# 96 gathered tokens instead of 80, a dense part 160 tokens wide, and another dealing out of the gather steps

## The chip, the cores and the metric

The kernel runs on one core of one Trainium2 chip. The time is that of one execution in device microseconds; lower is better. TensorE (PE) multiplies, VectorE (DVE) and ScalarE (ACT) do element work, GpSimd (POOL) issues the gathers, and the sequencer SP issues most of the plain loads. All transfers run on the core's 16 DMA engines.

## The reference, cut to what matters

The program is a small trunk of two layers on 256 tokens with 1024 features: a mixer, attention to a memory, and an expert part (`peer_ffn`), then a last norm. All is f32. The change concerns the expert part, in both layers alike. Each token has 8 heads, and each head picks 16 out of 16,384 experts, so 128 experts a token:

```python
eid = ...                                   # (tokens, 128) experts chosen
g = softmax(top) ...                        # (tokens, 128) their weights
act = gelu(einsum('td,ted->te', xb, u[eid]))
out = einsum('te,ted->td', g * act, v[eid])
```

`u` and `v` are tables of 16,384 rows of 1024 f32 per layer, 64 MiB each.

## The kernel before

**Two ways for the tokens.** The first `NG` = 80 tokens are *gathered*: for each, the 128 chosen rows of `u` and of `v` are fetched. The other `TD` = 176 tokens are *dense*: every expert is computed for them, and the weights of those that a token did not choose are zero. `GROUPS = ((0, 64), (64, 16))` divides the gathered tokens: 64 tokens whose 128 experts lie in 2 slots of 64 partitions, and 16 tokens with 8 slots of 16 partitions. One gather step takes one expert for each of 128 (token, slot) places, so a group of n tokens needs n steps with `u` and n with `v`; 80 + 80 = 160 steps a layer.

**The dense part** goes over the experts in 64 pairs of 128. For a `u` pair (`u_range`, matmuls at line 827) 1 MB of `peer_u` is loaded into a buffer `raw`, and 16 matmuls of 128 x 128 weights against the 176 dense tokens (`xd`) give the scores; ACT makes the gelu of them (line 833), for the first 20 pairs into `af`, for the others into `act`. The generator yields after each half pair. For a `v` pair (`v_pair`, matmuls at line 1134) 1 MB of `peer_v` is loaded, DVE multiplies the activations with the weights `gr` into `wt` (line 1130, three buffers), and 16 matmuls add to four banks `O`, which stay open through the whole stage. In the profile each f32 matmul is two instructions, 32 to a pair. `load` takes five `raw` buffers in turn; SP issues the loads.

**The gather steps** are the generator `gathered` (variable `bg`): each step issues an indirect load of 128 rows of 4 KB on POOL (`rows`, line 790; eight row buffers), and then one DVE instruction: with `u` rows a product with the token and its sum (line 797), with `v` rows a weighted add into `acc` (line 809, the first one line 807). The first 80 steps are those with `u`, the other 80 those with `v`. `turn[1]` counts the steps issued. At the end of a layer a matmul with `fold` adds the slots of `acc` up (line 1175).

**Order.** Within three stages DVE's order is the one written in the program, the rest is ordered by the compiler's planner. First, `choose` (top-k and the indices) is interleaved with `u` pairs: `interleave` calls one half pair for each 2.2 units of cost (`Q1`) that `choose` yields. What is left of the first 20 pairs runs with one gather step to each half pair (`steps`). Second, `spread` builds the dense weights from one-hot matmuls (line 1083), in groups of 16 dense tokens, 11 of them, and writes them to DRAM (`gd`); the next 20 `u` pairs run beside it, one half pair for each 1.7 units (`Q2`), and one gather step to two half pairs. Third, the v stage: 64 `v` pairs in the order of `order`, which are 6 of the first 20 (`NHEAD`, their weights already in `af`), then the others with the 14 remaining ones strewn in. Behind each `v` pair from 20 upwards one whole `u` pair follows, until the last 24 are used up. `gr` is read back from `gd` in pieces for 4 pairs (`weights_of`). After each `v` pair comes one gather step, after each fourth two: 80 in all. The steps that are then left run after the last pair, in `for _ in bg: pass`.

Of the kernel before, what the change touches and what calls it, by code (L numbers as in the profile page):

```python
# [28 lines left out]
NPAIR = 64  # L29
TG = 16  # L30
NFIRST = 20
NACT = 20

GROUPS = ((0, 64), (64, 16))
NG = sum(n for _, n in GROUPS)
TD = T - NG
NHEAD = 6
GQ = 4
Q1 = 2.2
Q2 = 1.7  # L40
# [28 lines left out]
def trunk(ctx: ExitStack, tc: tile.TileContext, a: dict, out: bass.AP, dbg=None):  # L69
# [37 lines left out]
    def bank():  # L107
        return ps.tile([P, 512], F32, name="b", tag="ps", bufs=2)
# [625 lines left out]
    def peer(l, sq, fill=None):  # L734
        with ExitStack() as es:
# [17 lines left out]
            gs_ = []  # L753
            for gn, (t0, n) in enumerate(GROUPS):
                xg = pp.tile([P, D], F32, name=f"xg{gn}", tag=f"ga{gn}")
# [15 lines left out]
            turn = [0, 0]  # L771


            def load(src):

                n = turn[0] % 5
                turn[0] += 1
                if n < 3:
                    raw = st.tile([P, 2048], F32, name="raw", tag="raw", bufs=3)
                else:  # L780
                    raw = cp.tile([P, 2048], F32, name="raw", tag=f"xT{n - 3}", bufs=1)
                nc.sync.dma_start(raw, src)
                return raw

            def rows(src, g, i):

                q = ("whi", "wlo")[turn[1] % 2]
                turn[1] += 1
                t = st.tile([P, D], F32, name="row", tag=q, bufs=4)
                nc.gpsimd.indirect_dma_start(t, None, src, bass.IndirectOffsetOnAxis(ap=g["gi"][:, i:i + 1], axis=0))  # L790
                return t

            def gathered():
                for g in gs_:
                    for i in range(g["n"]):
                        t = rows(u_rows, g, i)
                        nc.vector.tensor_tensor_reduce(t, t, g["xg"], 1.0, 0.0, OP.mult, OP.add, g["dots"][:, i:i + 1])  # L797
                        if i == g["n"] - 1:
                            nc.scalar.activation(g["dots"], g["dots"], AF.Gelu_apprx_tanh)
                            nc.vector.tensor_mul(g["gw"], g["gw"], g["dots"])  # L800
                        yield
                for gn, g in enumerate(gs_):
                    acc = g["acc"] = pp.tile([P, D], F32, name=f"acc{gn}", tag=f"ga{gn}")
                    for i in range(g["n"]):
                        t = rows(v_rows, g, i)
                        if i == 0:
                            nc.vector.tensor_scalar(acc, t, g["gw"][:, 0:1], None, op0=OP.mult)
                        else:
                            nc.vector.scalar_tensor_tensor(acc, t, g["gw"][:, i:i + 1], acc, op0=OP.mult, op1=OP.add)  # L809
                        yield  # L810
# [8 lines left out]
            def u_range(i, j):  # L819

                for i in range(i, j):
                    raw = load(a["peer_u"][l, i])
                    b = bank()
                    for c in range(2):
                        for k in range(KB):
                            o = c * 1024 + k * P
                            nc.tensor.matmul(b[:, c * TD:(c + 1) * TD], raw[:, o:o + P], xd[:, k], start=k == 0, stop=k == KB - 1)  # L827
                        if c == 1:
                            if i < NFIRST:
                                dst = af[:, 2 * i:2 * i + 2].rearrange("p c t -> p (c t)")  # L830
                            else:
                                dst = act[i] = pools["ex"].tile([P, 2 * TD], F32, name="act", bufs=NACT)
                            nc.scalar.activation(dst, b[:, :2 * TD], AF.Gelu_apprx_tanh)  # L833
                            done.append(dst)
                        yield
# [197 lines left out]
            us = u_range(0, NFIRST)  # L1033
            interleave(choose(), us, Q1)
            bg = gathered()

            def steps():
# [64 lines left out]
            us = u_range(NFIRST, NFIRST + NACT)  # L1102
# [10 lines left out]
            def weights_of(g):  # L1113
                if g < (NPAIR - NFIRST) // GQ:
                    gr[g] = vp.tile([P, TD // TG, GQ * 2 * TG], F32, name="gr", bufs=2)
                    nc.sync.dma_start(gr[g], gd[:, :, g * GQ * 2 * TG:(g + 1) * GQ * 2 * TG].rearrange("g p f -> p g f"))

            def v_pair(i, first, last):
                if i < NFIRST:
                    raw = load(a["peer_v"][l, i])  # L1120
                    wt = af[:, 2 * i:2 * i + 2]
                else:
                    g, j = divmod(i - NFIRST, GQ)
                    if j == 0:
                        weights_of(g + 1)
                    gv = gr[g][:, :, j * 2 * TG:(j + 1) * 2 * TG].rearrange("p g (c t) -> p c g t", c=2)
                    raw = load(a["peer_v"][l, i])
                    at = act.pop(i)
                    wt = vp.tile([P, 2, TD], F32, name="wt", bufs=3)
                    nc.vector.tensor_mul(wt.rearrange("p c (g t) -> p c g t", t=TG),  # L1130
                                         at.rearrange("p (c g t) -> p c g t", c=2, t=TG), gv)
                parts = [(c, j) for c in range(2) for j in range(KB)]
                for c, j in sorted(parts, key=lambda z: z[1]) if last else parts:
                    nc.tensor.matmul(O[j // 2][:, (j % 2) * TD:(j % 2 + 1) * TD], raw[:, c * 1024 + j * P:c * 1024 + (j + 1) * P],  # L1134
                                     wt[:, c], start=first and c == 0 and j % 2 == 0, stop=last and c == 1,
                                     skip_group_check=True)
                if last:
                    ready_sqrt(wt[:, 0, 0:1])


            order, late = list(range(NHEAD)), list(range(NHEAD, NFIRST))
            for i in range(NFIRST, NPAIR):
# [2 lines left out]
                    order.append(late.pop(0))  # L1145
            order += late
            us = u_range(NFIRST + NACT, NPAIR)
            with tc.manual_schedule(engines={nc.vector.engine}):
                for n, i in enumerate(order):
                    v_pair(i, n == 0, n == NPAIR - 1)  # L1150
                    if n == 1:
                        weights_of(0)
                    for _ in range(2 if n % 4 == 3 else 1):
                        next(bg, None)
                    if i >= NFIRST:
                        next(us, None)
                        next(us, None)
            for _ in bg:
                pass

# [58 lines left out]
    with ExitStack() as es:  # L1219
# [7 lines left out]
        left = [(l, c) for l in range(2) for c in range(8)]  # L1227
# [27 lines left out]
        dump("h_xa0", h)  # L1255
        fill(6)
    sq = peer(0, sq)
    dump("h_pe0", h)
    sq = odd_mixer(sq)
    dump("h_mix1", h)  # L1260
    with phase("kv1") as kp:
# [4 lines left out]
        sq = xattn(1, k1, v1, sq)  # L1266
    dump("h_xa1", h)
    sq = peer(1, sq)


# [101 lines left out]
```

## Time and profile before

| | |
|---|---|
| median of 3 runs | 2021.27 us (2020.26 to 2027.03) |
| the profiled execution | 2011.56 us, span 2009.3 us |
| PE busy | 1885.8 us, 94% of the span |
| DVE busy | 1090.7 us, 54% |
| POOL busy | 409.5 us, 20% |
| moved by DMA | 572.76 MB, 285 GB/s on the mean |
| mean granted clock of PE | 0.97 of full speed |

"Busy" is the time in which an engine worked on some instruction. Matmuls are pipelined, so the duration of one is longer than its distance from the next; a steady stream is better read from blocks of a known number of instructions in the chain of waits. The DMA share is the mean busy share of 16 engines and can exceed 1 by a little in a short window. Windows cut the span into stretches, and a stage is read from its own windows rather than from the means of the page.

### The profile page before, as it was taken

To read this page: it belongs to the slowest core of one execution; us is meant where nothing else is said; L and a number is where in the kernel's file an instruction comes from. 1 tells how busy PE (TensorE), PEld (TensorE's weight loads), DVE (VectorE), ACT (ScalarE), POOL (GpSimd) and SP (SyncE) were. 2 spreads that over 40 slices of the span, in tenths; PEclk is the share of its full clock that TensorE was granted. 3 is DMA by queue.
4 is the path that set the end of the run, shared out by engine and by line. 5 is a ranking of instruction groups with operands and counts; after the bars stand their busy time and mean duration, and the time that the engine had idled before them with its cause. 6 is when DMAs were issued, how large, how long until landed. Compare 5 with 4: busy or idle time off the path is not lost.

```text
span 2009.3 us, 33483 instructions
## 1 busy us (share of the span) xinstructions
PE 1885.8 (94%) x13818; PEld 1856.6 (92%) x13818; DVE 1090.7 (54%) x2494; ACT 447.2 (22%) x807; POOL 409.5 (20%) x360
## 2 busy tenths in 40 slices
PE   8999999999899999999299999999989999999992
PEld 7999999999899999999199899999989999999981
DVE  5765588676512222345878766985765121213467
ACT  6455442122100000000074455421221000000000
POOL 0000001432211111234600100014322121212344
PEclk9999999999999999999599999999999999999996
DMA  6554756999998899899863254579999889988997
GB/s 242 182 186 137 243 176 220 372 383 342 352 335 306 319 309 335 313 379 345 342 218 116 106 214 141 176 267 364 372 336 364 318 311 318 326 313 329 381 343 272
DMA packets 138631, 572.76 MB, mean 285 GB/s; under 512 B 12400, under 2 KB 47984, under 8 KB 94960
## 3 DMA queue, kind: packets, MB, share of 16 engines
q1 hardware_dynamic: 81008, 370.06, 50.6%
q0 software_dynamic: 46080, 167.79, 22.7%
q10 hardware_dynamic: 11392, 32.77, 4.3%
q8 instruction: 109, 1.79, 0.3%
q14 instruction: 42, 0.34, 0.0%
HBM read 549.48 MB, written 21.10 MB: 284 GB/s over the span
## 4 chain that ended last, share of the span: by engine, by line
PE 52%; issue 27%; DVE 8%; POOL 6%; DMA 5%; ACT 1%; DVEq 0%; POOLq 0%; ACTq 0%
PE O L1134 14%; PE b L148 13%; PE b L827 11%; PE b L163 7%; POOL row L790 6%; DMA row<-in_peer_ur_dram,gi 2%; DVE acc L809 2%; DMA row<-in_peer_v_dram,gi 1%; DMA kd<-kvs 1%; DVE row L797 1%; DMA vd<-kvs 1%; PE fb L869 1%; PE fb L312 1%; PE fa L281 1%; PE fb L552 1%
## 5 line engine op out<-in xcount | busy, mean ns | idle before, releaser
L827 PE MATMUL b<-xd,raw 128*128 128x176 f32 x4096 | 634.7, 315 | 0.7 <-ACT af L833 0.7
L827 PEld LDWEIGHTS b<-xd,raw 128*128 128x128 f32 x4096 | 618.1, 191 | 1.2 <-ACT af L833 1.2
L1134 PE MATMUL O<-wt,raw 128*128 128x176 f32 x2816 | 430.2, 313 | 0.0
L1134 PEld LDWEIGHTS O<-wt,raw 128*128 128x128 f32 x2816 | 422.6, 190 | 0.0
L1130 DVE TENSOR_TENSOR wt<-act,gr 128x352 f32<-128x352 f32 x88 | 46.2, 525 | 589.9 <-PE O L1134 563.7
L790 POOL DMA_INDIRECT row<-in_peer_ur_dram,gi x160 | 196.8, 1230 | 802.2 <-DVE dots L797 482.1
L790 POOL DMA_INDIRECT row<-in_peer_v_dram,gi x160 | 192.7, 1205 | 352.6 <-DVE acc L809 224.6
L148 PE MATMUL b<-xT,whi 128*128 128x256 f32 x1376 | 250.2, 283 | 2.8 <-DVE xT L129 2.4
L126 DVE TENSOR_TENSOR wlo<-raw,whi 128x1024 fp32r<-128x1024 f32 x158 | 191.2, 1220 | 101.6 <-ACT whi L125 100.9
L148 PEld LDWEIGHTS b<-xT,whi 128*128 128x128 f32 x1376 | 211.7, 189 | 5.2 <-DVE xT L129 3.8
L125 ACT ACTIVATE whi<-raw 128x1024 fp32r<-128x1024 f32 x158 | 166.1, 1060 | 217.7 <-PE b L148 117.9
L797 DVE CUSTOM_DVE_ANT_0 row<-row,xg 128x1024 f32<-128x1024 f32 x160 | 191.9, 1214 | 41.1 <-DMA row<-in_peer_ur_dram,gi 41.1
L809 DVE SCALAR_TENSOR_TENSOR acc<-row,gw,acc 128x1024 f32<-128x1024 f32 x156 | 200.1, 1283 | 7.7 <-DMA row<-in_peer_v_dram,gi 4.1
L1134 PE MATMUL O<-af,raw 128*128 128x176 f32 x1280 | 195.8, 313 | 0.0
L148 PE MATMUL b<-xT,wlo 128*128 128x256 f32 x688 | 192.5, 280 | 0.3 <-DVE wlo L126 0.3
L1134 PEld LDWEIGHTS O<-af,raw 128*128 128x128 f32 x1280 | 192.2, 190 | 0.0
L833 ACT ACTIVATE act<-b 128x352 f32<-128x352 f32 x88 | 40.9, 464 | 652.7 <-PE b L827 652.7
L148 PEld LDWEIGHTS b<-xT,wlo 128*128 128x128 f32 x688 | 129.7, 189 | 0.8 <-DVE wlo L126 0.5
L163 PE MATMUL b<-whi,y 128*128 128x256 f32 x512 | 89.4, 279 | 0.0
L1175 PE MATMUL b<-acc,fold 128*128 128x512 f32 x16 | 14.2, 1016 | 75.4 <-DVE acc L809 75.4
L1175 PEld LDWEIGHTS b<-acc,fold 128*128 128x128 f32 x16 | 4.2, 308 | 81.1 <-issue 44.3
L163 PEld LDWEIGHTS b<-whi,y 128*128 128x128 f32 x512 | 77.4, 188 | 0.4
(333 smaller groups left out, 1766.5 us busy)
## 6 DMA issues: line engine op xcount, KB each, us to landing
raw<-in_peer_u_dram SPq DMA_DIRECT2D x128, 1024.0 KB, 7.9
raw<-in_peer_v_dram SPq DMA_DIRECT2D x128, 1024.0 KB, 7.5
raw<-in_xattn_wkv_dram SPq DMA_DIRECT2D x16, 1024.0 KB, 5.0
raw<-in_peer_wq_dram SPq DMA_DIRECT2D x16, 1024.0 KB, 5.0
gd<-gs ACTq DMA_DIRECT2D x22, 704.0 KB, 8.7
gr<-gd SPq DMA_DIRECT2D x22, 704.0 KB, 9.7
raw<-in_odd_w_in_dram SPq DMA_DIRECT2D x15, 1024.0 KB, 4.9
raw<-in_even_w_in_dram SPq DMA_DIRECT2D x8, 1024.0 KB, 4.8
```

Source lines behind the costliest of these rows:

```text
L125: nc.scalar.activation(hi, src, AF.Copy)
L126: nc.vector.tensor_sub(lo, src, hi.bitcast(F32))
L148: nc.tensor.matmul(dst, w[j][p][:, k * P:(k + 1) * P], x[q][:, k, :], start=n == 0, stop=n == 3 * KB - 1)
L163: nc.tensor.matmul(dst, x[q][:, k, tb * P:(tb + 1) * P], wk[p][:, o:o + 256], start=n == 0, stop=n == 3 * KB - 1)
L281: nc.tensor.matmul(lg[:, tb * T:(tb + 1) * T], qT[p][:, 2 * hd + j, tb * P:(tb + 1) * P], kT[q][:, 2 * hd + j], start=n == 0, stop=n == 5)
L790: nc.gpsimd.indirect_dma_start(t, None, src, bass.IndirectOffsetOnAxis(ap=g["gi"][:, i:i + 1], axis=0))
L797: nc.vector.tensor_tensor_reduce(t, t, g["xg"], 1.0, 0.0, OP.mult, OP.add, g["dots"][:, i:i + 1])
L809: nc.vector.scalar_tensor_tensor(acc, t, g["gw"][:, i:i + 1], acc, op0=OP.mult, op1=OP.add)
L827: nc.tensor.matmul(b[:, c * TD:(c + 1) * TD], raw[:, o:o + P], xd[:, k], start=k == 0, stop=k == KB - 1)
L833: nc.scalar.activation(dst, b[:, :2 * TD], AF.Gelu_apprx_tanh)
L1130: nc.vector.tensor_mul(wt.rearrange("p c (g t) -> p c g t", t=TG), at.rearrange("p (c g t) -> p c g t", c=2, t=TG), gv)
L1134: nc.tensor.matmul(O[j // 2][:, (j % 2) * TD:(j % 2 + 1) * TD], raw[:, c * 1024 + j * P:c * 1024 + (j + 1) * P], wt[:, c], start=first and ...
```

## The change

The second group takes 32 tokens in 4 slots in place of 16 in 8. So 96 tokens are gathered, 192 steps a layer, and `TD` falls to 160: matmuls of 160 columns in the dense part, and 10 groups in `spread`. The v stage counts what PE still has to do, 64 `v` pairs and 24 `u` pairs less `NTAIL` = 3, and divides the gather steps that are left by that number; after each pair so many steps become due. The `u` pair of a turn now comes ahead of the turn's gather steps. The loop after the last pair stays in the program.

```diff
-GROUPS = ((0, 64), (64, 16))
+GROUPS = ((0, 64), (64, 32))
 NG = sum(n for _, n in GROUPS)
 TD = T - NG
 NHEAD = 6
+NTAIL = 3
...
             us = u_range(NFIRST + NACT, NPAIR)
+
+            left, todo = 2 * NPAIR - NFIRST - NACT - NTAIL, 2 * NG - turn[1]
+            due, per = 0.0, todo / left
             with tc.manual_schedule(engines={nc.vector.engine}):
                 for n, i in enumerate(order):
                     v_pair(i, n == 0, n == NPAIR - 1)
                     if n == 1:
                         weights_of(0)
-                    for _ in range(2 if n % 4 == 3 else 1):
+                    due += per
+                    if i >= NFIRST and next(us, "no") != "no":
+                        next(us, None)
+                        due += per
+                    while due >= 1:
+                        due -= 1
                         next(bg, None)
-                    if i >= NFIRST:
-                        next(us, None)
-                        next(us, None)
             for _ in bg:
                 pass
```

## Rows read from the trace of the kernel before

**Rows 1.** The profile's page of the kernel before, first part: busy time, share of the span and instructions of each engine.

```profile
PE 1885.8 (94%) x13818; PEld 1856.6 (92%) x13818; DVE 1090.7 (54%) x2494; ACT 447.2 (22%) x807; POOL 409.5 (20%) x360
```

**Rows 2.** The page's fifth part, the costliest groups of instructions, as the view of groups by line, engine and shape has them: line, engine, operation, out<-in, shapes, count | busy us, mean ns of one | idle time before it and what ended it.

```profile
L827 PE MATMUL b<-xd,raw 128*128 128x176 f32 x4096 | 634.7, 315 | 0.7 <-ACT af L833 0.7
...
L1134 PE MATMUL O<-wt,raw 128*128 128x176 f32 x2816 | 430.2, 313 | 0.0
...
L809 DVE SCALAR_TENSOR_TENSOR acc<-row,gw,acc 128x1024 f32<-128x1024 f32 x156 | 200.1, 1283 | 7.7 <-DMA row<-in_peer_v_dram,gi 4.1
...
L797 DVE CUSTOM_DVE_ANT_0 row<-row,xg 128x1024 f32<-128x1024 f32 x160 | 191.9, 1214 | 41.1 <-DMA row<-in_peer_ur_dram,gi 41.1
...
L552 PE MATMUL fb<-qd,kdd 128*128 128x128 f32 x96 | 12.0, 276 | 0.0
```

**Rows 3.** Windows by stage: start and end in us, length, then busy time (and instructions) of PE, PEld, DVE, ACT and POOL, granted PE clock, busy share of the DMA engines, GB/s. The first three are layer 0, the last two the v stage and the tail of layer 1.

```profile
406.00:537.00 131.00, 125.69 (x1037) 124.29 (x1036) 93.98 (x214) 30.02 (x65) 38.22 (x31) 0.97 0.96 361
537.00:957.00 420.00, 420.00 (x2817) 419.91 (x2816) 124.98 (x167) 14.56 (x31) 102.32 (x85) 1.00 0.92 331
957.00:1000.00 43.00, 4.06 (x7) 1.31 (x5) 38.84 (x33) 2.11 (x2) 29.94 (x28) 0.54 0.93 374
...
1534.40:1954.40 420.00, 419.77 (x2815) 419.50 (x2813) 125.36 (x167) 14.31 (x31) 101.60 (x84) 1.00 0.91 330
1954.40:1995.00 40.60, 4.32 (x5) 1.68 (x6) 38.27 (x31) 0.00 (x0) 26.46 (x25) 0.57 0.92 359
```

**Rows 4.** The chain of work that ended last, in order of time: start us, length us, what.

```profile
392.68 13.80 DMA row<-in_peer_ur_dram,gi
...
494.19 10.99 DMA row<-in_peer_ur_dram,gi
...
570.54 4.77 PE b L827 x32
575.31 4.77 PE O L1134 x32
...
1083.37 1.78 PE fb L552 x16
```

**Rows 5.** The waits of the SP queue from 537 to 957 us: who waited for whom, us in total, times, longest.

```profile
SPq L782 <- PE O L1134: 248.9, 59, 4.4
```

**Rows 6.** Timeline of the ends of both layers' expert parts, layer 0 first and the last two rows layer 1: start us, length us, engine, line, operation, out<-in, shapes, count [idle before it <- what ended it].

```profile
938.64 17.13 DVE L809 SCALAR_TENSOR_TENSOR acc<-row,gw,acc 128x1024 f32<-128x1024 f32 x13
...
947.47 9.71 PE L1134 MATMUL O<-wt,raw 128*128 128x176 f32 x64
...
972.28 1.01 POOL L790 DMA_INDIRECT row<-in_peer_v_dram,gi  x1 [0.31 <-issue]
...
999.87 2.08 PE L1175 MATMUL b<-acc,fold 128*128 128x512 f32 x2 [16.88 <-DVE acc L809]
...
1944.46 9.71 PE L1134 MATMUL O<-wt,raw 128*128 128x176 f32 x64
...
1994.39 2.08 PE L1175 MATMUL b<-acc,fold 128*128 128x512 f32 x2 [16.86 <-DVE acc L809]
```

**Rows 7.** Windows of line 797 alone (two instructions to each gather step, the product with its sum and the read of the sum): busy DVE time and count, clock, DMA share, GB/s.

```profile
341.00:406.00 65.00, 16.92 (x28) 0.96 0.91 353
406.00:537.00 131.00, 37.63 (x62) 0.97 0.96 361
```

**Rows 8.** The view of the DMA queues, of three stretches: first 370 to 410 us (packets and bytes in all; the queue of SP; the queue of POOL: packets, MB, share of 16 engines), then the issues from 840 to 930 us (count, KB each, us from issue to landing), last those of the next layer's weights from 940 to 990 us.

```profile
DMA packets 3200, 16.05 MB, mean 401 GB/s; under 512 B 350, under 2 KB 350, under 8 KB 2137
...
q1 hardware_dynamic: 1188, 8.69, 53.0%
q0 software_dynamic: 2010, 7.32, 47.1%
...
raw<-in_peer_v_dram SPq DMA_DIRECT2D x19, 1024.0 KB, 8.3
gr<-gd SPq DMA_DIRECT2D x2, 704.0 KB, 12.5
row<-in_peer_v_dram,gi POOLq DMA_INDIRECT x25, 9.1
...
raw<-in_odd_w_in_dram SPq DMA_DIRECT2D x2, 1024.0 KB, 8.8
```

**Rows 9.** Windows of 10 us: columns as in rows 3.

```profile
430.00:440.00 10.00, 10.00 (x85) 9.95 (x82) 6.25 (x16) 2.47 (x6) 1.87 (x2) 1.00 1.02 423
```

**Rows 10.** Windows of three stretches inside the v stages: columns as in rows 3.

```profile
840.00:930.00 90.00, 90.00 (x605) 90.00 (x604) 36.94 (x38) 0.00 (x0) 32.55 (x25) 1.00 0.99 375
1840.00:1930.00 90.00, 90.00 (x606) 90.00 (x605) 36.58 (x38) 0.00 (x0) 31.74 (x24) 1.00 0.99 378
...
600.00:800.00 200.00, 200.00 (x1343) 200.00 (x1342) 44.07 (x75) 8.83 (x20) 36.63 (x30) 1.00 0.90 316
```

**Rows 11.** Windows in which the granted clock is looked at: columns as in rows 3.

```profile
180.00:250.00 70.00, 65.82 (x568) 64.92 (x567) 38.62 (x59) 34.48 (x61) 1.17 (x6) 1.00 0.62 199
...
505.00:512.00 7.00, 3.74 (x23) 3.68 (x24) 6.80 (x12) 0.93 (x2) 3.18 (x3) 0.59 0.74 266
...
1000.00:1020.00 20.00, 17.42 (x111) 14.54 (x112) 11.82 (x23) 9.45 (x21) 0.00 (x0) 0.89 0.56 190
```

**Rows 12.** Timeline of PE around 508 us: columns as in rows 6.

```profile
507.93 0.27 PE L1083 MATMUL fa<-A,B 128*128 128x128 f16 x1 [4.97 <-DVE A L1072]
```

## The prediction

> **What bounds the kernel now.** I read the page first: TensorE is busy 94% of the span [rows 1], and the two dense lines of the expert part, 827 (scores from `peer_u`) and 1134 (sums into `O` from `peer_v`), are its largest groups [rows 2]. Then the windows by stage, for each layer: a first stage with the choice of experts and the spreading of their weights (341 to 537 us in layer 0), the v stage (537 to 957), and a tail up to 1000 us [rows 3]. In the v stage PE is busy all 420 us; the chain goes there from one block of 32 matmul instructions to the next, 4.77 us each, alternating lines 827 and 1134 [rows 4], and SP's loads wait for PE to free a buffer, not PE for loads [rows 5]. So PE bounds this stage: 88 pairs x 4.774 = 420.1 us. Beside it the DMA engines are already busy 0.92 of the time at 331 GB/s [rows 3]. The tail is another matter: the last matmul of line 1134 ends at 957.2 us, the fold that needs `acc` begins at 999.87, and between them DVE adds gathered rows and POOL issues one every 1.01 + 0.31 = 1.32 us [rows 6]. In layer 1 the same gap lasts from 1954.2 to 1994.39 us [rows 6]. That is 42.7 and 40.2 us of pure tail.
>
> **The dense part, 160 wide.** Each pair keeps its 32 instructions and has 16 columns less. The same kind of instruction, f32 with 128 columns, comes every 1.78 / 16 = 111 ns (line 552) [rows 2, 4]; with 176 columns every 4.77 / 32 = 149 ns [rows 4]. On the line between them 160 columns take 136.5 ns, 4.37 us for a pair, 0.40 us less. The bounds are nothing, if the weight load held the pace, and 9.1% by columns, 0.43 us; the 111 ns speak against the first, so I take 0.40. For the 88 pairs of the v stage PE would need 384.6 us instead of 420.1, for the 40 pairs before it 16 us less. Neither is a gain yet, because what PE consumes faster has to be fetched faster.
>
> **The gathers.** 96 tokens in groups of 64 and 32 make 96 steps with `peer_u` and 96 with `peer_v` per layer, 192 instead of 160; each fetches 128 rows of 4 KB, 0.524 MB. By the costs written in the code (46.7 in all, one half pair for each 2.2) 21 of the first 40 half pairs go to `choose`, so 19 steps follow in `steps`; `spread` gave 39 / 2 = 19 more and gives, with 10 groups of 16 tokens instead of 11, 35 / 2 = 17. So 38 were issued ahead of the v loop, and 36 will be. By 537 us DVE had done 45, half the 28 + 62 instructions of line 797 [rows 7]: the 38 and the 7 of the six head pairs, whose weights lie ready in `af`. The new loop has to deal out 192 - 36 = 156 over 2 x 64 - 20 - 20 - 3 = 85 pairs, 1.835 a pair, and all are out when three pairs are left; the six head pairs bring 11, so 47 done at the start of the v stage. After it 145 come, where 115 came in v stage and tail together.
>
> The engines can carry that. DVE has 30 more such steps of 1.21 or 1.28 us [rows 2], 38 us, in a stretch in which it is busy 125 of 420 us; POOL 30 x 1.32 = 40 us more beside 102 of 420 [rows 3]. In the DVE queue the gather steps stand ahead of the next `wt` product, and PE waits for that if a row comes late; what covers it is three `wt` buffers and eight row buffers.
>
> **What the DMA engines must move** is the sum that decides. In v stage and tail of layer 0 they moved 420 x 0.331 + 43 x 0.374 = 155.1 MB [rows 3], of which some 2.1 MB are two weight loads of the next layer [rows 8]: 153.0 MB. The change adds 30 x 0.524 = 15.7 MB and takes a group off `gr`, 1/11 of 11 x 0.72 MB: 168.0 MB. In PE's 384.6 us that is 437 GB/s. The fullest 10 us stretch among these rows, at 430 us, has 423 GB/s [rows 9]. So the v stage becomes bound by DMA, and its time is bytes over the rate of a full queue. For that rate there are two nearest rows. At 370 to 410 us loads and gathers overlap with a row so late that DVE waits 13.8 us for it [rows 4], and 401 GB/s flow, 53% of engine time for the loads, 47% for the gathers [rows 8], nearly the shares of the new v stage (54 to 46 by bytes). There are no `gr` loads there, whose pieces are 512 bytes. At 840 to 930 us there are, 2 beside 19 loads and 25 gathers [rows 8], as dense as in the new stage: 375 GB/s, and 378 in layer 1, with the engines 0.99 busy and PE not held up [rows 10], so this is a lower bound or close to one. I take 390, between the two: 168.0 / 0.390 = 431 us, and 5 us for the last three pairs, which have no gathers beside them and go at PE's pace: 436 us. PE end to fold then costs nothing of note, for `acc` is ready. Before, v stage and tail took 462.9 and 460.2 us. **Gain 27 + 24 = 51 us.** At 376 GB/s it is 20 us, at 401 it is 76.
>
> Here a rule of the Trainium skill speaks against the change. "DMA: Bandwidth & Descriptors", section Bandwidth, says that between HBM and SBUF the HBM side binds at about 358 GB/s for each core, though its own measurements with the other core idle go to 425. The 401 GB/s of this trace [rows 8] are above the rule; with 358 the sum would end near no change.
>
> **The first stage.** From 406 to 537 us PE is busy 125.7 of 131 us [rows 3]. Its 40 pairs get 16 us shorter, and one of 11 groups of spreading goes. But the engines move 361 GB/s at 0.96 there, and two waits for a gathered row, 13.8 and 11.0 us, lie on the chain [rows 4]; two steps more than before are to be done by its end (47 against 45). Bounds: 3 us lost (the two steps at 1.32 us, if the queue takes nothing more), and 20 us won (PE's 16 and the group's 2 to 4). I take 8 in each layer, 16 us, nearer to nothing because of those waits.
>
> **The clock.** In the tail PE stands still and its granted clock falls to 0.54 [rows 3], the lower level being 1.2 GHz; the next 20 us still have 0.89 on average [rows 11], about 4.4 us of them at half clock. Without the tail that goes: 2.5 us a layer, 5 us, between nothing and 9. The six matmuls with `win` in place of ten, the smaller `act` and `wt`, all beside PE's stream, I cost at nothing; should they surface, it is 1 to 2 us. SP's order of loads stays as it is.
>
> **Sum:** 51 + 16 + 5 = 72 us off the profiled execution, 2011.6 to 1939.6 us. The median of the runs is 2021.3, 9.7 us above that execution; I carry the difference over: 1949, say 1950 us.
>
> **The rivals.**
> A, DMA flows at 415 to 420 GB/s and PE nearly stays the bound: 168.0 / 0.420 + 5 = 405 us, 58 + 55 us, with the whole 20 us of the first stage twice and 5: 158 us, 1863. For it: single stretches of 423 [rows 9]. Against: none lasts, and `gr` is in the mix. Chance 0.16.
> B, slower: the queues don't reach 390 when three kinds of transfer mix. At 600 to 800 us, 316 GB/s take 0.90 of the engines' time [rows 10], 351 for a full one. Then the stage takes 168.0 / 0.351 + 5 = 484 us, 21 and 23 us more than v stage and tail did; PE is held, and with 8 us from first stage and 4 from the clock the kernel ends at 2054. It decides from 359 GB/s downwards, where 168.0 / 0.359 + 5 = 473 us eat up the 21 us of the rest. Against it: 375 and 378 with PE never held [rows 10]. Chance 0.13. Between 356 and 362 GB/s nothing is left of the gain either way (2015 to 2027): 0.08. By the 358 GB/s of the Trainium skill's page above that middle case would be the likeliest.
> C, the clock: PE now waits about 0.5 us per pair for data. If such waits cost the granted clock, as one of 4.97 us did (0.59 over 505 to 512 us) [rows 11, 12], PE falls behind DMA as soon as the mean is under 384.6 / 431 = 0.89; at 0.75 the stage takes 513 us and the kernel some 80 us more, 2100. Against: 180 to 250 us, where PE lacks 4.2 of 70 us in short waits, at 1.00 [rows 11]. Chance 0.05. The page "TensorE: Matmul & The Clock Gate" of the Trainium skill, section "HAM oscillation — how this bites in real kernels", describes such a loop of DMA waits and falling clock; by it C would weigh more if the waits came in long pieces.
> D, the change doesn't do all it says: gathers lag by a full set of eight rows and more when PE ends, ten steps x 1.32 = 13 us of tail left in each layer: 1976. Chance 0.08.
>
> **How the numbers follow.** The forecast, 380 to 405 GB/s, has 0.50. Faster: it, A and D, 0.74; same (within 0.3%, 6 us, what a measurement can tell): 0.08; slower: B and C, 0.18. Low end: 405 GB/s and 15 us of first stage, 43 + 40 + 30 + 6 = 119 us, 1902; I take 1900. High end: 360 GB/s with 4 us of first stage and nothing of the clock, 472 us, 9 and 12 us lost less 8: 2034; I take 2030. A's far part lies below it, B's and C's above.
>
> **What would show it.** In the changed profile: pairs of 4.37 us where nothing holds them; the v stage about 436 us long, PE with waits for `raw` or `wt` in it; DMA 0.98 and more at 380 to 400 GB/s over the whole v stage; no stretch with PE idle before line 1175's counterpart; the clock at 1.00 through it. The forecast falls if DMA shows idle time while PE waits, if the rate is outside 376 to 405, if the first stage gets longer, or if rows are still added after the last pair.

## The result, and the profile after

The changed kernel takes 1945.9 us in the median of its runs, the kernel before 2020.8 us in the same ones: 0.9627 of the time, 95% interval 0.9603 to 0.9651. The forecast was 1950 us. The profiled executions have spans of 1944.3 and 2009.3 us, 65.0 us apart. The total is close to the forecast, but the parts that add up to it are not those of the forecast, as the stages show.

Windows of the changed kernel, columns as in rows 3: the v stage of layer 0, its part until 937 us and the rest, and the same three of layer 1.

```profile
527.50:967.50 440.00, 397.28 (x2818) 395.69 (x2818) 199.96 (x242) 13.73 (x31) 166.44 (x142) 0.95 0.99 389
527.50:937.00 409.50, 366.78 (x2594) 365.21 (x2594) 195.51 (x235) 12.58 (x28) 164.39 (x139) 0.94 1.03 407
937.00:967.50 30.50, 30.50 (x226) 30.49 (x225) 4.45 (x7) 1.14 (x3) 2.05 (x3) 1.00 0.45 158
1490.35:1929.20 438.85, 398.19 (x2818) 396.61 (x2817) 199.88 (x241) 13.73 (x31) 170.94 (x138) 0.95 0.98 389
1490.35:1899.00 408.65, 367.99 (x2596) 366.41 (x2595) 195.57 (x236) 12.58 (x28) 170.20 (x137) 0.94 1.03 407
1899.00:1929.20 30.20, 30.20 (x224) 30.20 (x223) 4.31 (x6) 1.14 (x3) 0.74 (x1) 1.00 0.40 147
```

Where PE was busy without a gap before and DMA 0.92 [rows 3], DMA now is full (407 GB/s, with a busy share of 1.03: the share goes above 1 here over 409 us, and not only in a short window) and PE has gaps; then come 30 us in which PE works through and DMA is 0.40 to 0.45 busy. The tail has gone. In the chain of the changed kernel, in order of time, the fold (line 1182, before 1175) follows the last block of line 1136 (before 1134) at once, where 42.7 us lay between them [rows 6]; a pair takes 4.35 us, and a load of 23 us stands in the chain:

```profile
599.14 4.35 PE b L829 x32
...
612.21 23.04 DMA raw<-in_peer_u_dram
635.39 7.15 PE b L829 x32
...
900.62 66.83 PE O L1136 x480
967.46 1.72 PE b L1182 x4
...
1290.19 2.51 DVE big L971 x4
...
1490.35 30.43 PE O L1136 x224
```

Two lines of the kernel before go with it, the same row of `big` (chain) and the first `v` matmul of layer 1 (timeline):

```profile
1322.89 2.51 DVE big L969 x4
...
1533.95 2.25 PE L1134 MATMUL O<-af,raw 128*128 128x176 f32 x14
```

With them the 65.0 us divide up. The first stage gives 537.0 - 527.5 = 9.5 us in layer 0 and (1533.95 - 1322.89) - (1490.35 - 1290.19) = 10.9 in layer 1. From the first `v` matmul to the fold it was 462.9 and 460.4 us and is 440.0 and 438.8: 22.9 + 21.6. All else gives 0.1 us.

PE's gaps come in pieces. Timeline of the changed kernel (columns as in rows 6):

```profile
635.39 7.15 PE L829 MATMUL b<-xd,raw 128*128 128x160 f32 x32 [5.82 <-DMA raw<-in_peer_u_dram]
...
646.92 0.49 DVE L1132 TENSOR_TENSOR wt<-act,gr 128x320 f32<-128x320 f32 x1 [12.24 <-PE O L1136]
...
648.83 1.67 POOL L791 DMA_INDIRECT row<-in_peer_v_dram,gi  x1 [10.86 <-DVE dots L799]
```

PE waits 5.8 us for a load. DVE, three products ahead, then waits for PE, and POOL for DVE. While POOL issues next to nothing, the loads get ahead again: from 612 to 626 us the gathers' queue took 75% of the engines' time and the loads' queue 29%, from 636 to 650 us it was 35% and 66%. In each v stage there are five such waits of 5.5 to 7.9 us, 47 to 52 us apart, and some 117 us after the fifth a last one, of 10.7 us in layer 0 and 8.9 in layer 1. Around them PE's granted clock falls (0.84 over 620 to 640 us) while DMA goes on at over 400 GB/s; windows as above:

```profile
620.00:640.00 20.00, 14.18 (x88) 13.96 (x87) 11.38 (x20) 0.44 (x1) 12.48 (x10) 0.84 1.04 405
640.00:660.00 20.00, 20.00 (x146) 20.00 (x146) 8.31 (x15) 0.91 (x3) 5.73 (x5) 0.98 1.02 417
```

### The profile page after: what moved, and what is told of

The parts are those of the page before. It is cut to its first block, busy times and chain, and to the rows that moved or that the text cites. A ratio compares the mean times of both kernels' runs of the same rounds, so it can differ in the third digit from the quotient of the medians.

```text
span 1944.3 us, 33584 instructions
## 1 busy us (share of the span) xinstructions
PE 1795.2 (92%) x13738; PEld 1767.6 (91%) x13738; DVE 1157.1 (60%) x2562; ACT 439.0 (23%) x799; POOL 496.3 (26%) x424
## 4 chain that ended last, share of the span: by engine, by line
PE 60%; DMA 21%; DVE 9%; issue 6%; POOL 1%; ACT 1%; another core or an unknown queue 0%; DVEq 0%; SPq 0%; ACTq 0%; POOLq 0%
PE O L1136 20%; PE b L149 14%; PE b L829 13%; DMA raw<-in_peer_u_dram 8%; DMA raw<-in_peer_v_dram 8%; PE b L164 6%; DMA row<-in_peer_ur_dram,gi 3%; POOL row L791 1%; DMA kd<-kvs 1%; DVE row L799 1%; DMA vd<-kvs 1%; PE fb L871 1%; PE fb L313 1%; PE fb L553 1%; PE fa L282 1%
## 5 line engine op out<-in xcount | busy, mean ns | idle before, releaser
L829 PE MATMUL b<-xd,raw 128*128 128x160 f32 x4096 | 597.2, 307 | 40.6 <-DMA raw<-in_peer_u_dram 36.3
L791 POOL DMA_INDIRECT row<-in_peer_ur_dram,gi x192 | 241.9, 1260 | 614.2 <-DVE dots L799 285.4
L1136 PE MATMUL O<-wt,raw 128*128 128x160 f32 x2816 | 392.6, 299 | 0.0
L791 POOL DMA_INDIRECT row<-in_peer_v_dram,gi x192 | 234.2, 1220 | 341.3 <-DVE acc L811 262.2
L799 DVE CUSTOM_DVE_ANT_0 row<-row,xg 128x1024 f32<-128x1024 f32 x192 | 230.6, 1218 | 108.6 <-DMA row<-in_peer_ur_dram,gi 104.0
L1132 DVE TENSOR_TENSOR wt<-act,gr 128x320 f32<-128x320 f32 x88 | 43.2, 491 | 383.1 <-PE O L1136 346.4
L811 DVE SCALAR_TENSOR_TENSOR acc<-row,gw,acc 128x1024 f32<-128x1024 f32 x188 | 241.2, 1283 | 16.0 <-DMA row<-in_peer_v_dram,gi 11.7
L1136 PE MATMUL O<-af,raw 128*128 128x160 f32 x1280 | 191.9, 312 | 47.1 <-DMA raw<-in_peer_v_dram 47.1
L835 ACT ACTIVATE act<-b 128x320 f32<-128x320 f32 x88 | 38.4, 437 | 687.1 <-PE b L829 486.3
L164 PE MATMUL b<-wlo,y 128*128 128x256 f32 x256 | 70.6, 278 | 0.0
```

Source lines behind the costliest of these rows:

```text
L164: nc.tensor.matmul(dst, x[q][:, k, tb * P:(tb + 1) * P], wk[p][:, o:o + 256], start=n == 0, stop=n == 3 * KB - 1)
```

## Experiments

Theory 1: the v stage lasts as long as its bytes need at 407 GB/s, or as long as PE's pairs, whichever is more, plus what PE still has to do when the gathers are through. Theory 2: not bytes but the order in DVE's, POOL's and SP's queues and the falling clock hold PE up. Times are medians, with the ratio to the kernel before in the same comparison and its 95% interval.

**Each half of the change alone.** First the new dealing with the old sizes:

```diff
-GROUPS = ((0, 64), (64, 32))
+GROUPS = ((0, 64), (64, 16))
```

> The new dealing out of the gather steps on the old sizes: 80 gathered tokens, 176 dense ones. Theory 1 (the v stage takes the longer of PE's pairs and bytes over 407 GB/s): 153 MB need 376 us, PE's 88 pairs need 420, so PE bounds, the v stage takes 420 to 423 us in each layer and no tail follows; 40 us a layer less than the kernel before, some 1935 us, below the changed kernel. Theory 2 (gather steps ahead of the next wt product in DVE's queue, loads held up in SP's queue and the clock that falls in PE's waits make the stage long, not the bytes): PE waits here too, the v stage takes 440 us or more, 1970 us or more.

1934.4 us, 0.9564 (0.9540 to 0.9588): better than the whole change. The v stages are some 20 us shorter than in the changed kernel, and the first stage of layer 0 is 10 us longer. Windows of its v stages:

```profile
537.80:957.80 420.00, 420.00 (x2817) 420.00 (x2817) 161.75 (x195) 14.56 (x31) 136.15 (x111) 1.00 0.95 367
...
1496.60:1916.70 420.10, 420.10 (x2818) 420.10 (x2817) 161.74 (x195) 14.56 (x31) 133.08 (x107) 1.00 0.94 365
```

PE has no gap, although all 122 remaining steps are dealt out beside its pairs by the same code as in the change. At this density, 1.44 steps a pair where the change has 1.84, queue order alone makes no wait.

Then the kernel before with 96 tokens and the old dealing, `GROUPS = ((0, 64), (64, 32))` only:

> 96 gathered tokens and a dense part of 160 with the old dealing out: one step for each v pair, two for each fourth, the rest after the last pair. Theory 1: 80 steps in the v stage leave it bound by PE, 385 to 390 us; 76 steps are left, of which about 66 run after PE's end at 1.32 us, 87 us; with 10 us less in the first stage each layer takes as long as before: 2010 to 2025 us. Theory 2 (the gain is that of the narrower matmuls): 1945 to 1960 us.

2009.3 us, 0.9934 (0.9915 to 0.9953), just under theory 1's range. Windows of its v stage and tail:

```profile
528.40:914.00 385.60, 382.61 (x2809) 381.80 (x2808) 119.67 (x183) 13.30 (x30) 102.27 (x86) 1.00 0.97 362
914.00:1000.00 86.00, 6.02 (x13) 3.05 (x12) 83.75 (x68) 2.65 (x4) 62.36 (x60) 0.50 0.98 387
```

The v stage is PE's 385 us, as the forecast has it for 160 columns, and the 86 us behind it eat that up. The new sizes (narrower dense part, more gathers) are worth next to nothing by themselves; theory 2's 1945 us is out.

**Bytes or steps.** The changed kernel with as many steps, POOL instructions and DVE work, but rows of 2 KB:

```diff
-nc.gpsimd.indirect_dma_start(t, None, src, ...)
+nc.gpsimd.indirect_dma_start(t[:, :512], None, src, ...)   # src viewed as half rows
...
-nc.vector.scalar_tensor_tensor(acc, t, ...)
+for hs in (slice(0, 512), slice(512, 1024)):
+    nc.vector.scalar_tensor_tensor(acc[:, hs], t[:, :512], ...)
```

The product with a `u` row and the first add of a group are halved in the same way; those lines are left out here.

> The changed kernel with gathered rows of 2 KB in place of 4 KB, as many steps, and two half instructions on DVE for each whole one: half of each gathered row is left out, and the other half stands for it. Theory 1: 92 MB of loads and half of 76 MB of rows need 336 us at 407 GB/s, PE 385, so the v stage takes 385 to 390 us and no clock falls in it: some 1835 to 1850 us. Theory 2: POOL's and DVE's queues are as long as before, the v stage stays near 440 us, 1940 us.

1828.9 us in one run, a little below what was expected. (92 and 38 MB are 130 MB, which need 319 us at 407 GB/s and not 336; PE's 385 is the longer either way.) Windows around its v stages; that of layer 0 lasts from 525.1 to 908.7 us, 383.6 us:

```profile
520.00:910.00 390.00, 389.22 (x2859) 388.32 (x2858) 213.24 (x436) 14.97 (x33) 146.54 (x141) 1.00 0.93 346
1429.00:1812.00 383.00, 382.59 (x2817) 382.32 (x2816) 212.74 (x435) 13.86 (x31) 145.32 (x138) 1.00 0.93 346
```

DVE is busier than in the changed kernel (213 against 200 us), POOL issues as often, and PE has next to no gaps: it was the bytes. The price of a step from the other side: 16 steps a layer left out (the second group takes 24 of its 32 experts a slot, `todo` is less by 16).

> The changed kernel (NTAIL 3) with 8 of the second group's 32 experts a slot left out, so 16 gather steps a layer fewer, 176; that part of the sum is missing. Theory 1: 8.4 MB a layer less, at 407 GB/s 20.6 us a layer; the v stage goes from 440 to 419 to 422 us, 1903 to 1910 us. If the steps cost by their place in DVE's or POOL's queue (16 x 1.3 us beside PE's work), nothing is gained where PE doesn't wait for them: 1935 us or more.

1909.1 us, 0.9445 (0.9426 to 0.9464), within what theory 1 gave. The v stages last 423.9 and 421.6 us, of which the first is above theory 1's 419 to 422, so a step cost 1.0 to 1.1 us, a little under its 1.29 us at 407 GB/s. The end with PE alone stayed 26.5 us long. The v stages as windows:

```profile
522.60:946.50 423.90, 395.58 (x2818) 394.22 (x2817) 181.64 (x221) 13.85 (x31) 156.75 (x128) 0.96 0.97 383
...
1468.30:1889.90 421.60, 393.97 (x2817) 392.39 (x2816) 181.66 (x221) 13.85 (x31) 152.95 (x124) 0.97 0.97 384
```

**The end of the stage.** `NTAIL = -4` instead of 3:

> The changed kernel with NTAIL = -4 in place of 3: 1.70 steps a pair, seven left for the time after the last pair's product. Theory 1: the 30 us at the end in which PE works on with the DMA engines at 0.4 shrink to 12 to 18 us, since the gathers last longer and the loads are ahead sooner; the v stage goes from 440 to 424 to 430 us, 1915 to 1925 us. Theory 2: the waits stay as many, the seven steps come on top: 1945 to 1955 us.

1913.3 us, 0.9453 (0.9417 to 0.9489), a little below theory 1's range, and on another occasion:

> NTAIL = -4 once more, beside the two that vary it: 1908 to 1918 us.

1918.0 us, 0.9503 (0.9478 to 0.9528). Windows of the first of them, whose v stage begins at 525.2 us and so lasts 425.3 us:

```profile
527.00:950.60 423.60, 394.20 (x2806) 393.05 (x2805) 199.83 (x243) 13.29 (x30) 170.92 (x141) 0.96 1.02 403
527.00:925.00 398.00, 368.60 (x2618) 367.44 (x2617) 184.41 (x229) 12.15 (x27) 163.71 (x134) 0.95 1.03 407
925.00:950.60 25.60, 25.60 (x190) 25.60 (x190) 15.43 (x14) 1.14 (x3) 7.21 (x8) 1.00 0.89 353
```

Rate and clock are those of the changed kernel (the second of them has 403 GB/s in its full part); what went is the idle of DMA in the last 26 us (353 GB/s instead of 158). With `NTAIL = -10`:

> NTAIL = -10: 1.64 steps a pair, twelve left behind the last pair's product. Theory 1: with NTAIL = -4 the queues are already full to the end (403 GB/s over the whole v stage against 407 in its full part), so at most 4 us a layer are to be had, and the twelve steps last some 16 us, about as long as PE still works: within 10 us of NTAIL = -4 on either side. If the end of PE's work were still the cost, it would gain 10 us or more.

1921.4 us, 0.9496 (0.9482 to 0.9509), no different from the second run of -4. (The 156 steps over 98 turns are 1.59 a pair and leave sixteen, where the expectation has 1.64 and twelve; after the last product DVE in fact added 18 rows.) Its timeline shows that the end has now gone over to the gathers, PE's last fold waiting for `acc`:

```profile
939.61 1.88 PE L1182 MATMUL b<-acc,fold 128*128 128x512 f32 x4
953.78 2.07 PE L1182 MATMUL b<-acc,fold 128*128 128x512 f32 x2 [12.29 <-DVE acc L811]
```

**The pieces of `gr`.** On `NTAIL = -4`, `GQ = 11` instead of 4:

> NTAIL = -4 and gr read back for 11 pairs at a time instead of 4, in pieces of 1408 bytes instead of 512, the same bytes. If the small pieces cost rate, as the forecast took it (390 against 401 GB/s without them, 12 us a layer), it gains 10 to 25 us. If they cost next to nothing at full queues (407 GB/s were reached with them), it stays within 6 us of NTAIL = -4, or loses a few us where the first, larger read holds up the first product.

1901.8 us, 0.9405 (0.9391 to 0.9419), 16 us below -4 with 512-byte pieces in the same comparison. Windows, and the v stage of that second run of -4 and its full part for comparison:

```profile
526.50:946.50 420.00, 390.32 (x2818) 389.41 (x2817) 200.23 (x243) 13.86 (x31) 164.22 (x143) 0.96 1.01 408
526.50:829.00 302.50, 272.82 (x1953) 271.91 (x1952) 135.48 (x180) 10.99 (x26) 114.91 (x100) 0.95 1.02 412
829.00:920.00 91.00, 91.00 (x672) 91.00 (x671) 46.77 (x48) 1.72 (x2) 39.61 (x33) 1.00 1.01 404
...
524.20:951.70 427.50, 395.94 (x2818) 394.26 (x2817) 199.63 (x243) 13.75 (x31) 175.96 (x143) 0.96 1.01 399
524.20:906.00 381.80, 350.60 (x2497) 348.89 (x2495) 175.37 (x220) 12.60 (x28) 160.93 (x131) 0.96 1.02 403
```

412 GB/s in the long part instead of 403, and PE without a gap from 829 us on. The edit makes the pieces larger and the reads fewer (8 instead of 22) at once; which of the two counts was not taken apart. The same edit where PE bounds the stage, on the 80 tokens of the first experiment:

> 80 gathered tokens with the new dealing (as the first experiment) and gr in pieces of 1408 bytes. Theory 1: there PE bounds the v stage without a wait (420 us), so what eases the DMA engines gains nothing: within 5 us of 1934 us. If the small pieces cost time in another way (SP's queue, DVE's waits for gr), it gains 10 us or more, as it did with 96 tokens.

1928.9 us, 0.9601 (0.9580 to 0.9622) beside a kernel before of 2010.9 us on that occasion: no gain over 0.9564. So the pieces cost only where DMA bounds, as theory 1 says. `NTAIL = -4` with `GQ = 11` is the fastest version here that does all the work, below both kernels.

## Why the prediction was right, and where not

- **The 160 columns**: 4.35 us a pair against 4.37 forecast; with nothing in the way 385 us, as experiment 2 showed.
- **The bound goes from PE to DMA, and the tail goes**: right, and shown by the half rows (half the row bytes, next to no gap) and the dealing alone (bytes that fit into PE's time, no gap).
- **The v stage, 436 us forecast, 440 and 439 measured**: right in the sum by luck, for two errors cancel. The first is the rate. 390 GB/s was too low: full queues gave 407, so 168 MB take 413 us, not 431. (The mean over the whole v stage is 389, but as a mean of 407 and 158.) The row at 840 to 930 us (375) was no full queue, for PE had no gap there and asked for no more; that its DMA share was 0.99 misled me. The other row, 370 to 410 us with 401 GB/s, was one in which an engine did wait for DMA, and alone it would have given 419 us. DVE's wait there was 10.2 us long, as the timeline of the kernel before has it; the forecast's 13.8 us are the length of the load:

```profile
406.51 1.23 DVE L797 CUSTOM_DVE_ANT_0 row<-row,xg 128x1024 f32<-128x1024 f32 x1 [10.16 <-DMA row<-in_peer_ur_dram,gi]
```

- **The end of the v stage** is the second error. "5 us for the last three pairs" had no ground, since three pairs at 4.37 us are 13, and it took 30 us. DVE deals the steps out up to three products ahead of PE, and among these pairs lies one that needs no product (`af`). With the three pairs of `NTAIL` that makes seven when PE is counted, and 30.5 / 4.35 = 7.0. `NTAIL = -4` filled these with transfers and took 12 to 15 us off each v stage.
- **`gr` in small pieces as a cost**: 12 us a layer in the forecast; larger pieces, in fewer reads, gave 8 us a layer back. The cost was there, but on a higher rate.
- **First stage**: 16 us forecast, 20.4 measured; experiment 1 starts its v stage at 537.8 us and experiment 2 at 528.4, so it comes with the new sizes. How much of it is PE and how much the eleventh group was not taken apart.
- **Clock**: 5 us forecast, nothing measured. In the 20 us behind the fold the granted clock is now 1.00 instead of 0.89 [rows 11], but PE is busy 17.4 us of them in both kernels, and what follows takes the same time: 323.0 us from fold to the next layer's `big` before, 322.7 after. What PE waits for there stays open.
- **The total**: 51 + 16 + 5 = 72 us were forecast for the profiled execution, and 44.5 + 20.4 + 0.1 = 65.0 came. That the medians still met the forecast within 4 us is luck too. The forecast added 9.7 us, by which the profiled execution of the kernel before lay below its median, and that of the changed kernel (1946.2 us) lies at its median.
- **The signs**: 389 GB/s over the whole v stage lie in the 376 to 405 that the forecast named, but the 407 of its full part do not, and the clock was 0.95 there where the forecast has 1.00.
- **Rivals**: A would have needed 420 GB/s; 412 to 413 is the most that a long stretch gave, with larger pieces. B's 351 didn't come. C came about in part: the waits gathered into pieces of 6 us and more, and the clock fell to 0.95 on the mean, but that is above the 0.89 from which it would have counted, and DMA stayed full meanwhile. That these falls cost nothing is argued from this; no run took them away alone. D didn't come.
- What the forecast didn't look at is either half alone. As the change stands, its sizes cost: with 80 tokens the new dealing is done within PE's 420 us (0.9564), with 96 the DMA engines need longer than that (0.9627). With the end of the stage filled the 96 tokens come out ahead (`NTAIL = -4`: 0.9453 and 0.9503), and with the larger `gr` pieces as well by more (0.9405).

The Trainium skill ("DMA: Bandwidth & Descriptors", section Bandwidth) gives about 358 GB/s for a core when both cores of an HBM domain stream, and up to 425 in its measurements with the other core idle. This kernel, on one core, went past the 358: 407 GB/s over 409 us.

## What to carry to other kernels

Before work is shifted from a full engine to the DMA engines, add up the bytes of that stage and divide by the rate of a stretch in which somebody waits for DMA; a stretch in which nobody waits gives the demand, not the limit, even if DMA looks 0.99 busy. Deal out filler work by the work that the bounding engine still has, and count from that engine's place in time: a queue that runs some pairs ahead of it ends that many pairs early. Try the parts of a combined change one at a time, for here one part alone was better than both.

## What the runs showed that I had not expected

The busy share of the DMA engines hides headroom: 0.99 went with 375 GB/s [rows 10] and 1.03 with 407 over 409 us. The waits under a full DMA queue came bunched, most of them some 6 us about every 48 us, rather than 0.5 us for each pair; by the shares of the two queues around one of them, gathers and loads take turns in getting ahead. The reads of `gr` are 22 x 0.655 = 14.4 MB of 603 MB, 2.4% of the traffic; larger pieces for them gave 0.8% of the time.
